# Two stacked blocks of diffusion-style layers: the order of a projection, of norms and of modulation sums is changed

## The chip, the cores and the metric

One core of a Trainium2 chip runs the whole program in one launch. The time is the device time in microseconds (us); each kernel is run three times and the median counts. Engines: TensorE (PE: matmuls; PEld: its weight loads), VectorE (DVE), ScalarE (ACT), GpSimd (POOL), SyncE (SP, which issues all DMAs here).

## What is computed

The input is an image sequence x (256 tokens of 1024), a context of the same size, and two modulation vectors c and c_ctx. The first block has two layers, the second has two layers of another kind (NSA, with its compressed keys and values, pooling, convolution and forgetting attention in four branches). Cut to what the change touches:

```python
for i in range(2):                                  # first block
    sh1, sc1, g1, sh2, sc2, g2 = split(silu(c) @ ada_w[i] + ada_b[i], 6)
    csh1, csc1, cg1, csh2, csc2, cg2 = split(silu(c_ctx) @ ada_w[i] + ada_b[i], 6)
    h  = rmsnorm(x,  norm_mix[i]) * (1 + sc1)  + sh1
    hc = rmsnorm(xc, norm_mix[i]) * (1 + csc1) + csh1
    y, yc = diff_attention(...) if i == 0 else neighbourhood_attention(...)
    x  = x + g1 * y
    x  = x + g2 * conv_ffn(rmsnorm(x, norm_ffn[i]) * (1 + sc2) + sh2)     # D_FF = 2816
    if i == 0:                                      # the context is dropped after layer 0
        xc = xc + cg1 * yc
        xc = xc + cg2 * conv_ffn(rmsnorm(xc, norm_ffn[i]) * (1 + csc2) + csh2)
x = rmsnorm(x, norm_out)
for l in range(2):                                  # second block
    proj = rmsnorm(x, norm_g[l]) @ w_in[l]          # q, kv, gates, pool, conv, fox, merge
    kc = compress(proj.k_c); vc = compress(proj.v_c)  # silu(blocks @ w1 + b1) @ w2 + b2
    ...
```

## The kernel before, in words

**Layout and precision.** The residual stream xT lies in SBUF with features on partitions: 8 chunks (kc, or m for an output block) of 128 features, 256 image columns and 256 context columns. Every large matmul is done three times on a high and a low part of both operands (`mm3` L331, `mm3r` L1055: high x high, high x low, low x high). So each weight block is loaded by SP, its high part is made by ScalarE and its low part by VectorE or GpSimd (`wload` L320, `split` L306: ScalarE at L311, the low part at L314). A count `nsplit` over all calls of `split`, with `pool_every`, picks which low parts go to GpSimd: with 3, each third one.

**Order.** A planner puts the instructions of each engine in an order of its own by a simulated timeline; the order of the program text is their priority. Three tools bind it. `keep_in_program_order` pins one instruction behind the one that the text has before it on its engine. `manual_schedule` makes the named engines issue in the order of the text. A hand-written plan (`chain` L701 with `tick`, `step`, `flush`) counts triples of matmuls: after n[0] triples it issues the mean of a norm (`norm_mean` L496), after n[1] more its broadcast (`norm_bcast` L519) and the eight scaled chunks (`norm_half`), and pins the matmuls around them.

**Norms.** The squares are made by ScalarE and added up, chunk by chunk (`norm_add` L466: square at L474, sum at L476, by the engine in "eng", the last by VectorE) or, at the front, in pairs of chunks (`norm_pairs` L479: squares at L484, three sums at L486). Two small matmuls with ones give the mean, GpSimd does the power -0.5 (L516), two more matmuls spread 1/rms over the partitions (L525), and ScalarE copies it (`nbc`). Then `norm_apply` L533 makes each chunk's scaled input: a product on VectorE (`nt`, L543), the high part on ScalarE (L544), the low part on VectorE (L545). Where the feed-forward needs the norm late, its first blocks multiply a scaled but not yet normalised input (`scale_fz` L567 into `fz`, tile v in the trace) and 1/rms is put in afterwards (`up_z` L574, `ffn` with `pre`).

**Modulation.** The six vectors per layer come in two ways. Some pieces go through TensorE in the first layer (`ada_piece` L373: 8 matmuls, a copy, two transposes, a reduce and a sum on VectorE, and a gain at L411). The other seven vectors, 56 rows of 1024 weights with two sums each (c and c_ctx), are 112 sums on VectorE (`ada_steps` L415; tile junk, L436, with a row `araw` loaded per two sums and the vectors `cb` loaded once for each feed-forward). A count of sums is given out at each up block (with 2 from block 2 on) and at each down block (3 and 4 in turn) of the feed-forward of layer 0, and what is left at the up blocks of layer 1's.

**Stages around the change.** `layer0` L721: loads, 14 warm-up matmuls, the image's norm, and the values' projection, which for each of 8 chunks adds 4 accumulators of image rows (12 matmuls of 512 columns: the triple of one accumulator before that of the next) and, from chunk 1 on, 2 of context rows; then 8 heads (`diff_head` L1096; the head's output norm ends in L1141 and the transposes at L1146), the output projection in two halves of heads (`wo` L836, the first half inside the turn of head 6), the residuals, and the norm of the feed-forward. In the second half of the output projection blocks 0 to 2 take image and context together, blocks 3 to 7 first the image, then the norm of the image, then the context (`late`). `ffn` L584 has two halves of 11 up blocks and 8 down blocks each. `layer1` L953 is the neighbourhood attention; its output projection fills `fz`, and three up blocks (`up_z`) run on it before the second feed-forward. `hybrid` L1169 is a layer of the second block; `compress_in` L1479 copies the keys and values into blocks on VectorE (`blk`, four sums), loads two weight tiles and does 32 small matmuls; `compress_out` L1510 ends the compression. Between them stands the values' projection.

## Time and profile before

| | |
|---|---|
| runs | 1619.59, 1617.31, 1611.44 us (median 1617.31) |
| the profiled execution | 1616.63 us, its span 1614.7 us, mean granted clock 0.988 |
| PE busy | 1563.8 us (97%), 10390 matmuls |
| DVE busy | 1096.7 us (68%) |
| ACT busy | 771.0 us (48%) |
| POOL busy | 527.9 us (33%) |
| HBM | 250.21 MB read, 156 GB/s over the span |

The rows below count from the start of the span. Busy times are sums of instruction times of one engine in a stretch. The granted clock (PEclk) is TensorE's clock in parts of full speed, averaged over the stretch. An arrow out<-in names the program's tiles; "x3" behind a row of a timeline is the number of like instructions drawn together.

### The profile page before, as it was taken

How to read it: one execution, taken by the hardware profiler on the slowest of the kernel's cores; microseconds unless marked ns; L12 is line 12 of the kernel's file. 1: busy time of each engine (PE TensorE's matmuls, PEld its weight loads, DVE VectorE, ACT ScalarE, POOL GpSimd, SP SyncE). 2: the span in 40 equal slices, each digit the busy share in tenths (PEclk: the TensorE clock that was granted, in tenths of full speed). 3: DMA queues.
4: the chain of work that ended last, by engine and by line, in shares of the span. 5: the costliest groups of instructions: out<-in, count | busy, mean ns of one | idle time of the engine just before them, and what ended most of it. 6: DMA issues, size and time to landing. Idle time of an engine off the chain costs nothing.

```text
span 1614.7 us, 26688 instructions
## 1 busy us (share of the span) xinstructions
PE 1563.8 (97%) x10390; PEld 1364.8 (85%) x10390; DVE 1096.7 (68%) x1927; ACT 771.0 (48%) x1386; POOL 527.9 (33%) x500
## 2 busy tenths in 40 slices
PE   7999999899999999999999987999999999999998
PEld 5777677788888888878777987999899999899998
DVE  4656677687999995343444898567657667757665
ACT  3445454454322443244545563565654445555443
POOL 2122331341100111251323654665455223552222
PEclk9999999999999999999999999999999999999999
DMA  7523233234467541243231555447335555425552
GB/s 298 218 78 128 108 131 118 83 140 169 165 212 262 209 160 61 93 153 118 96 115 35 208 186 190 183 160 260 131 106 186 207 191 208 156 92 178 188 198 90
DMA packets 49485, 252.98 MB, mean 157 GB/s; under 512 B 5072, under 2 KB 8144, under 8 KB 31568
## 3 DMA queue, kind: packets, MB, share of 16 engines
q1 hardware_dynamic: 49360, 251.28, 43.3%
q8 instruction: 82, 1.34, 0.3%
q14 instruction: 43, 0.35, 0.1%
HBM read 250.21 MB, written 1.05 MB: 156 GB/s over the span
## 4 chain that ended last, share of the span: by engine, by line
PE 86%; DVE 8%; issue 2%; ACT 2%; POOL 1%; DMA 1%; SPq 0%; DVEq 0%; POOLq 0%; ACTq 0%
PE acc L335 12%; PE acc L338 12%; PE acc L339 12%; PE S L338 9%; PE S L339 9%; PE S L335 9%; PE S L1084 3%; DVE wlo L314 2%; PE misc L383 1%; PE misc L1131 1%; PE misc L1026 1%; PE S L1058 1%; PE S L1061 1%; DVE junk L436 1%; PE S L1062 1%
## 5 line engine op out<-in xcount | busy, mean ns | idle before, releaser
L311 ACT ACTIVATE whi<-raw 128x1024 fp32r<-128x1024 f32 (+2 forms) x374 | 373.9, 1007 | 433.8 <-PE S L338 174.1
L314 DVE TENSOR_TENSOR wlo<-raw,whi 128x1024 fp32r<-128x1024 f32 (+3 forms) x305 | 373.3, 1225 | 164.8 <-ACT whi L311 164.3
L335 PE MATMUL acc<-hhi,whi 128*128 128x256 f32 (+1 forms) x824 | 271.1, 329 | 1.9 <-DVE u L618 1.4
L338 PE MATMUL acc<-hlo,whi 128*128 128x256 f32 (+1 forms) x824 | 270.9, 329 | 0.7 <-DVE hlo L545 0.6
L339 PE MATMUL acc<-hhi,wlo 128*128 128x256 f32 (+1 forms) x824 | 268.7, 327 | 1.4 <-DVE wlo L314 1.4
L314 POOL TENSOR_TENSOR wlo<-raw,whi 128x1024 fp32r<-128x1024 f32 (+1 forms) x69 | 166.5, 2414 | 193.1 <-ACT whi L311 187.8
L339 PE MATMUL S<-hhi,wlo 128*128 128x256 f32 (+1 forms) x560 | 179.5, 321 | 1.8 <-DVE wlo L314 1.8
L335 PE MATMUL S<-hhi,whi 128*128 128x256 f32 (+1 forms) x560 | 178.1, 318 | 1.4 <-ACT whi L311 1.4
L338 PE MATMUL S<-hlo,whi 128*128 128x256 f32 (+1 forms) x560 | 179.0, 320 | 0.0
L335 PEld LDWEIGHTS acc<-hhi,whi 128*128 128x128 f32 x824 | 154.9, 188 | 24.5 <-issue 9.7
L338 PEld LDWEIGHTS acc<-hlo,whi 128*128 128x128 f32 x824 | 154.9, 188 | 18.8 <-issue 5.0
L339 PEld LDWEIGHTS acc<-hhi,wlo 128*128 128x128 f32 x824 | 154.9, 188 | 15.4 <-DVE wlo L314 1.6
L436 DVE SCALAR_TENSOR_TENSOR junk<-araw,cb 128x1024 bf16<-128x1024 f32 x112 | 148.9, 1330 | 4.6 <-ACT cb L424 4.3
L624 POOL TENSOR_TENSOR u<-u,u 128x256 f32<-128x256 f32 (+1 forms) x46 | 59.2, 1288 | 273.8 <-ACT u L623 261.5
L335 PEld LDWEIGHTS S<-hhi,whi 128*128 128x128 f32 x560 | 105.9, 189 | 9.7 <-ACT whi L311 1.8
L339 PEld LDWEIGHTS S<-hhi,wlo 128*128 128x128 f32 x560 | 105.8, 189 | 9.5 <-DVE wlo L314 2.4
L338 PEld LDWEIGHTS S<-hlo,whi 128*128 128x128 f32 x560 | 105.9, 189 | 8.4
L1457 POOL TENSOR_TENSOR macc<-macc,mm 128x256 f32<-128x256 f32 x48 | 49.2, 1026 | 162.6 <-DVE mm L1455 162.6
L335 PE MATMUL acc<-hlo,whi 128*128 128x256 f32 x288 | 81.5, 283 | 1.1 <-DVE kA L1236 1.1
L338 PE MATMUL acc<-hhi,whi 128*128 128x256 f32 x288 | 81.9, 284 | 0.0
L339 PE MATMUL acc<-hlo,wlo 128*128 128x256 f32 x288 | 81.2, 282 | 0.0
L335 PE MATMUL S<-ghi,whi 128*128 128x256 f32 (+1 forms) x231 | 76.3, 333 | 4.9 <-DVE xT L638 4.8
(416 smaller groups left out, 3744.8 us busy)
## 6 DMA issues: line engine op xcount, KB each, us to landing
raw<-in_up SPq DMA_DIRECT2D x44, 1024.0 KB, 4.8
raw<-in_mg SPq DMA_DIRECT2D x32, 1024.0 KB, 5.1
araw<-in_adav SPq DMA_DIRECT2D x56, 512.0 KB, 4.3
raw<-in_t SPq DMA_DIRECT2D x24, 1024.0 KB, 4.8
raw<-in_down SPq DMA_DIRECT2D x32, 704.0 KB, 4.1
raw<-in_ada SPq DMA_DIRECT2D x16, 1024.0 KB, 4.9
raw<-in_aqk SPq DMA_DIRECT2D x8, 1024.0 KB, 5.6
raw<-in_bqk SPq DMA_DIRECT2D x8, 1024.0 KB, 4.8
```

Source lines behind the costliest of these rows:

```text
L311: nc.scalar.activation(hi[:, :n], raw, AF.Copy)
L314: eng.tensor_tensor(lo[:, :n], raw, hi[:, :n].bitcast(F32), op=ALU.subtract)
L335: first = nc.tensor.matmul(ps, wh, x[0], start=start, stop=False)
L338: nc.tensor.matmul(ps, wh, x[1], start=False, stop=False)
L339: nc.tensor.matmul(ps, wl, x[0], start=False, stop=stop)
L383: nc.tensor.matmul(ps[32 * j : 32 * j + 32, 0:256], self.cs[:, 4 * r + j, :], raw[:, 4 * r + j, :], start=(r == 0), stop=(r == 1), tile_po ...
L436: nc.vector.scalar_tensor_tensor(junk, self.araw, 1.0, self.acb[0][:, c, :], op0=ALU.mult, op1=ALU.mult, accum_out=self.ada[l][:, v, k, c ...
L624: nc.gpsimd.tensor_tensor(us[0], us[0], us[1], op=ALU.mult)
L1026: nc.tensor.matmul(o[64 * j : 64 * j + 64, :], v[:, t, (2 * h + j) * 64 : (2 * h + j) * 64 + 64], pT[:, j, t, :], start=(t == 0), stop=(t ...
L1058: first = nc.tensor.matmul(ps, x[0], w[0], start=start, stop=False)
L1084: self.nc.tensor.matmul(sps[j][:, :n], q[a][r, qs], k[b][r, ks], start=(e == 0), stop=(e == 2))
L1457: nc.gpsimd.tensor_tensor(acc, acc, m, op=ALU.add)
```

## The change

Six places. (1) The image half of xT comes in four loads instead of two. The image's norm, the first two modulation pieces and the first two chunks of the values' projection of the image rows run under `manual_schedule` on TensorE, ScalarE and VectorE; the twelve matmuls of a chunk go product by product (high x high for all four accumulators first), piece 1's transposes stand behind the first four; the low weights of chunk 0 and the sums of squares of the context half are VectorE's, and the first square of the context is pinned. `ada_piece` is cut in two for this. (2) Six of the eight output blocks of the first half of heads stand behind head 7 instead of head 6. (3) In the second half the image blocks 3 to 7 are pinned in the order of the text, and the context's scaled chunks come after 16 more triples instead of 5. (4) Before the second feed-forward, the norm is a `chain` (mean after 14 triples, the rest after 8 more), and the first two up blocks do their last two input chunks at their end. (5) All 112 sums of the modulation are given out in the first feed-forward. (6) `compress_in` stands behind the values' projection instead of before it.

```diff
...
     def ada_piece(self, p, raw=None):
+        self.ada_columns(p, *self.ada_parts(p, raw))
+    def ada_parts(self, p, raw=None):
         nc = self.nc
...
         nc.scalar.activation(part, ps[:, 0:256], AF.Copy)
+        return ps, part
+    def ada_columns(self, p, ps, part):
+        nc = self.nc
         for v in range(2):
...
         s["k"] += 1
-    def norm_pairs(self, s, x, pool, eng=None):
+    def norm_pairs(self, s, x, pool, pin=False):
         nc = self.nc
...
             sq = self.t(pool, [P, 512], "p", bufs=4).rearrange("p (e t) -> p e t", e=2)
-            nc.scalar.activation(sq, x[:, 2 * k : 2 * k + 2, :], AF.Square)
+            first = nc.scalar.activation(sq, x[:, 2 * k : 2 * k + 2, :], AF.Square)
+            if pin and k == 0:
+                self.tc.keep_in_program_order(first)
             if k:
-                (eng or nc.vector).tensor_tensor(s["pair"], s["pair"], sq, op=ALU.add)
+                nc.vector.tensor_tensor(s["pair"], s["pair"], sq, op=ALU.add)
             else:
...
         return ws, pss
+    def up_z_late(self, l, js, late):
+        res = []
+        for j in js:
+            ws = self.wload(self.i["up"][l, j], [1024, 1024])
+            pss = [self.acc5((P, T + 2)) for _ in range(2)]
+            res.append((ws, pss))
+            for which in range(2):
+                self.proj(pss[which], ws[which], self.fz[0], self.fz[1], T + 2, kcs=range(KC - late))
+        for ws, pss in res:
+            for which in range(2):
+                self.proj(pss[which], ws[which], self.fz[0], self.fz[1], T + 2, kcs=range(KC - late, KC))
+        return res
     def ffn(self, l, halves, h_hi, h_lo, sts, mid=None, pre=(), bc=None):
...
                 for jj in range(first, NFH):
                     end = up(s * NFH + jj, jj, ghi, glo)
-                    if s * NFH + jj >= 2:
+                    if l == 0:
                         self.ada_steps(fp, 2, end)
...
                     if l == 0:
-                        self.ada_steps(fp, 3 + m % 2, None)
+                        self.ada_steps(fp, 4 + s, None)
                     if s == 1 and m >= 6 and len(halves) == 2:
...
             def load_half(h):
-                for q in range(2):
-                    nc.sync.dma_start(
-                        self.xT[:, 4 * q : 4 * q + 4, T * h : T * h + T], i["xin"][h, :, 4 * q : 4 * q + 4, :]
-                    )
+                n = 2 if h == 0 else 4
+                for q in range(0, KC, n):
+                    nc.sync.dma_start(self.xT[:, q : q + n, T * h : T * h + T], i["xin"][h, :, q : q + n, :])
             stage = [self.t(hp, [P, 2, 2048], n) for n in ("ohi", "olo")]
...
             self.warm(14)
-            self.norm_pairs(sts[0], self.xT[:, :, 0:T], hp)
-            mean = self.norm_mean(sts[0])
-            self.ada_piece(0, ada[0])
-            bcs = [self.norm_bcast(self.norm_rstd(sts[0], mean)), None]
             hhi, hlo = self.new_h()
             v = self.t(hp, [P, 4128], "v")[:, 0:4096].rearrange("p (t e) -> p t e", t=4)
-            def vacc(vps, kc, w, o):
-                for (tt, hf), ps in vps.items():
-                    c = slice(tt * P, tt * P + P)
-                    f = slice(o + 512 * hf, o + 512 * hf + 512)
-                    self.mm3r(ps, (hhi[:, kc, c], hlo[:, kc, c]), (w[0][:, f], w[1][:, f]), kc == 0, kc == KC - 1)
+            def vacc(vps, kc, w, o, between=None):
+                for e, (a, b) in enumerate(((0, 0), (0, 1), (1, 0))):
+                    for (tt, hf), ps in vps.items():
+                        c = slice(tt * P, tt * P + P)
+                        f = slice(o + 512 * hf, o + 512 * hf + 512)
+                        nc.tensor.matmul(
+                            ps, (hhi, hlo)[a][:, kc, c], w[b][:, f], start=(kc == 0 and e == 0), stop=(kc == KC - 1 and e == 2)
+                        )
+                    if between and e == 0:
+                        between()
             def vout(vps, h0=0):
...
             vps = {(0, 0): self.acc(), (0, 1): self.acc(), (1, 0): self.sb(), (1, 1): self.sb(), (2, 0): self.sb(), (3, 0): self.misc()}
-            ws = []
-            for kc in range(KC):
+            bcs, ws = [None, None], []
+            front = {k: a for k, a in vps.items() if k[0] < 2}
+            with self.tc.manual_schedule(engines={nc.tensor.engine, nc.scalar.engine, nc.vector.engine}):
+                self.norm_pairs(sts[0], self.xT[:, :, 0:T], hp)
+                rstd = self.norm_rstd(sts[0])
+                parts = self.ada_parts(0, ada[0])
+                bcs[0] = self.norm_bcast(rstd)
+                self.ada_columns(0, *parts)
+                for kc in range(2):
+                    hi = self.t(self.st, [P, 1024], "whi", F32R, bufs=self.wb)
+                    lo = self.t(self.st, [P, 1024], "wlo", F32R, bufs=self.wb)
+                    ws.append((hi, lo))
+                    nc.scalar.activation(hi, avs[kc], AF.Copy)
+                    tmp = self.t(self.nrm, [P, T], "nt", bufs=5)
+                    A, B = self.nA[0][0][:, kc, 0:1], self.ada[0][:, 0, kc, 0:1]
+                    h = hhi[:, kc, 0:T], hlo[:, kc, 0:T]
+                    nc.vector.scalar_tensor_tensor(tmp, self.xT[:, kc, 0:T], A, bcs[0], op0=ALU.mult, op1=ALU.mult)
+                    nc.scalar.activation(h[0], tmp, AF.Identity, bias=B)
+                    nc.vector.tensor_tensor(lo, avs[kc], hi.bitcast(F32), op=ALU.subtract)
+                    nc.vector.scalar_tensor_tensor(h[1], tmp, B, h[0].bitcast(F32), op0=ALU.add, op1=ALU.subtract)
+                    if kc == 0:
+                        parts = self.ada_parts(1, ada[1])
+                    vacc(front, kc, ws[kc], 0, (lambda: self.ada_columns(1, *parts)) if kc == 0 else None)
+            for kc in range(1, KC):
                 if kc % 2 == 0 and kc:
...
                     avs[kc], avs[kc + 1] = raw[:, 0:1024], raw[:, 1024:2048]
-                self.pool_every = 1 if kc < 1 else 0
-                ws.append(self.split(avs[kc], 1024))
-                self.norm_half(0, 0, 0, kc, hhi, hlo, bcs[0])
-                vacc({k: a for k, a in vps.items() if k[0] < 2}, kc, ws[kc], 0)
-                if kc == 0:
-                    self.ada_piece(1, ada[1])
-                    continue
-                if kc == 1:
-                    self.norm_pairs(sts[1], self.xT[:, :, T : 2 * T], hp, nc.gpsimd)
+                if kc > 1:
+                    ws.append(self.split(avs[kc], 1024))
+                    self.norm_half(0, 0, 0, kc, hhi, hlo, bcs[0])
+                    vacc(front, kc, ws[kc], 0)
+                else:
+                    self.norm_pairs(sts[1], self.xT[:, :, T : 2 * T], hp, True)
                     bcs[1] = self.norm_bcast(self.norm_rstd(sts[1]))
...
                     wo_load(0, 1)
-                    for m in (4, 5, 6, 7):
+                    for m in (4, 5):
+                        wo(0, m, (0, 1), self.acc)
+                if h == 7:
+                    for m in (6, 7):
                         wo(0, m, (0, 1), self.acc)
...
             for m in late:
+                self.pin = True
                 wo(1, m, (0,), self.acc5)
...
             for m in late:
                 wo(1, m, (1,), self.acc5)
-            self.chain((8, 5), 0, 1, 1, sts[1], hh)
+            self.chain((8, 16), 0, 1, 1, sts[1], hh)
             pre = [self.up_z(0, 0)]
...
             hhi, hlo = self.new_h()
-            bc = self.normed(1, 1, (0,), [st2], (hhi, hlo))
-            pre = [self.up_z(1, j) for j in range(2)]
-            pre.append(self.up_z(1, 2, (self.acc5, self.misc)))
+            done = []
+            self.chain((14, 8), 1, 1, 0, st2, (hhi, hlo), done)
+            pre = self.up_z_late(1, range(2), 2)
+            pre.append(self.up_z(1, 2, (self.misc, self.misc)))
+            self.flush()
+            bc = done[0]
         if self.stop == "l1a":
...
         q = [rope2(chunk(3 + c), 0, f"q{c}") for c in range(2)]
-        part = self.compress_in(l, hp, kvT)
         vps = [self.misc() for _ in range(2)]
...
             nc.scalar.activation(vs[:, tt, :], vps[tt][:, 0:400], AF.Copy, scale=rstd[:, tt : tt + 1])
-        kcT, vc = self.compress_out(l, hp, part, wcp)
+        kcT, vc = self.compress_out(l, hp, self.compress_in(l, hp, kvT), wcp)
         gate = t(hp, [P, 2, 12], "gate")
...
```

## Rows read from the trace of the kernel before

**Rows 1.** The page, part 4: chain that ended last, by engine
```profile
PE 86%; DVE 8%; issue 2%; ACT 2%; POOL 1%; DMA 1%; SPq 0%; DVEq 0%; POOLq 0%; ACTq 0%
```

**Rows 2.** TensorE's waits: line <- releaser: us in total, times, longest
```profile
PE misc L1146 <- DVE p L1141: 4.9, 2, 3.5
PE S L335 <- DVE xT L638: 4.8, 1, 4.8
...
PE misc L525 <- POOL nrstd L516: 3.0, 2, 2.8
```

**Rows 3.** Stretches: length, busy (instructions) of PE, PEld, DVE, ACT, POOL; PEclk; DMA
```profile
10.00:24.88 14.88, 8.86 (x61) 5.77 (x61) 7.31 (x13) 6.02 (x11) 6.88 (x5) 0.89 1.03 405
24.88:38.20 13.32, 12.79 (x88) 8.60 (x88) 5.33 (x14) 4.63 (x9) 0.70 (x1) 0.87 0.64 263
285.00:310.00 25.00, 20.13 (x134) 15.47 (x134) 10.46 (x30) 8.30 (x22) 2.94 (x5) 0.86 0.31 115
325.00:333.00 8.00, 5.24 (x31) 5.24 (x32) 6.11 (x16) 3.17 (x8) 4.33 (x5) 0.79 0.36 135
880.00:910.00 30.00, 26.71 (x187) 25.03 (x188) 23.72 (x28) 16.44 (x29) 19.84 (x12) 0.89 0.38 140
930.00:937.00 7.00, 4.86 (x26) 4.45 (x26) 6.89 (x9) 5.71 (x10) 4.52 (x3) 0.76 0.05 18
955.00:1010.00 55.00, 43.79 (x326) 41.65 (x326) 49.89 (x68) 20.58 (x34) 25.46 (x14) 0.94 0.52 179
1020.00:1100.00 80.00, 80.00 (x681) 80.00 (x680) 51.11 (x82) 50.62 (x89) 51.20 (x32) 1.00 0.50 175
1120.00:1130.00 10.00, 7.74 (x85) 7.37 (x84) 9.28 (x17) 2.17 (x4) 5.74 (x7) 1.00 0.58 217
1368.00:1380.00 12.00, 10.43 (x127) 9.65 (x126) 11.91 (x22) 2.96 (x6) 7.72 (x8) 1.00 0.27 89
400.00:604.00 204.00, 204.00 (x893) 167.52 (x892) 201.37 (x305) 72.83 (x94) 20.30 (x13) 1.00 0.58 202
604.00:680.00 76.00, 76.00 (x346) 62.86 (x345) 35.21 (x53) 28.07 (x44) 14.15 (x14) 1.00 0.23 80
```

**Rows 4.** Timeline of the front: start, length, instruction, idle before it
```profile
8.26 2.29 DVE L486 TENSOR_TENSOR p<-p,p 128x512 f32<-128x512 f32 x3 [7.14 <-ACT p L484]
8.39 1.15 ACT L484 ACTIVATE p<-xT 128x512 f32<-128x512 f32 x2 [0.16 <-DMA xT<-in_xin]
...
16.41 0.16 DVE L411 SCALAR_TENSOR_TENSOR nA<-ada,vec 128x2 f32<-128x2 f32 x1
16.67 0.49 DVE L543 SCALAR_TENSOR_TENSOR nt<-xT,nA,nbc 128x256 f32<-128x256 f32 x1
...
20.04 3.96 POOL L486 TENSOR_TENSOR p<-p,p 128x512 f32<-128x512 f32 x3 [3.69 <-ACT p L484]
...
21.48 1.20 DVE L411 SCALAR_TENSOR_TENSOR nA<-ada,vec 128x2 f32<-128x2 f32 x1
22.71 1.57 DVE L543 SCALAR_TENSOR_TENSOR nt<-xT,nA,nbc 128x256 f32<-128x256 f32 x1
...
24.88 0.52 PE L1058 MATMUL acc<-whi,hhi 128*128 128x512 f32 x1 [3.84 <-ACT hhi L544]
```

**Rows 5.** Timeline of VectorE around the second feed-forward
```profile
902.09 1.57 DVE L476 TENSOR_TENSOR naccx<-naccx,nsq 128x256 f32<-128x256 f32 x1 [0.61 <-ACT nsq L474]
...
955.83 2.61 DVE L365 TENSOR_TENSOR glo<-u,ghi 128x256 fp32r<-128x256 f32 x1
```

**Rows 6.** Matmuls on the scaled input v, up to the mean (PE alone)
```profile
894.88:904.10 9.22, 7.23 (x36) 0.73 0.31 114
```

**Rows 7.** The sums (tile junk) on VectorE; each counts two instructions
```profile
380.00:500.00 120.00, 67.33 (x103) 1.00 0.56 199
500.00:620.00 120.00, 57.51 (x90) 1.00 0.53 185
940.00:1002.00 62.00, 25.00 (x32) 1.00 0.58 204
```

## The prediction

> **What bounds the kernel now.** I read the page's chain first: TensorE holds 86% of the chain that ended last, VectorE 8% [rows 1]. So no step gains by making another engine's work shorter; time can come only from places where TensorE stands still or runs at the lower of its two clock levels. I then read TensorE's waits [rows 2]: none is long (the three shown are among the four largest), and they stand at few places of the program. Last I cut the span into stretches around these places [rows 3]. Each row gives what TensorE did in a stretch and the granted clock; the row from 1020 to 1100 us is the measure of a full stage (681 matmuls of 256 columns in 80 us, 0.1175 us each, at 2.4 GHz). A granted clock of 0.87 over 13.32 us means that 2 x 0.13 x 13.32 = 3.5 us ran at 1.2 GHz, which loses at most half of that, 1.7 us. Each drop to 1.2 GHz follows a stretch with idle TensorE, so a filled gap gives back part of it too.
>
> **Part 1, the front (10 to 38 us).** Four steps.
> (a) The image half is loaded in four transfers instead of two. The last squares start when the second transfer lands, 8.39 us, and two squares and two sums follow it before the mean [rows 4]. With quarters only one square and one sum (0.6 + 0.7 us by the same rows) stand behind the last landing: 0.9 us less, if the last quarter lands when the half did. Two more issues come on SP's queue ahead of all later loads; those queue up anyway (405 GB/s from 10 us on [rows 3]), so I cost that at nothing, and keep a loss of 0.9 us, the gain turned round, as the lower end. The Trainium skill, "DMA: Bandwidth & Descriptors", section "Rules for kernel authors", asks for at least 1 MiB a transfer and speaks against this step; by it the step would give nothing, and the sum below would be 0.9 us smaller. No row here shows a quarter's landing.
> (b) Between the first and the second chunk of the values' projection TensorE stands 3.84 us, until the high part of chunk 1's input is there. Before it VectorE did a gain in 1.20 us and a product in 1.57 us; both lie under GpSimd's three sums of squares of the context half, 20.04 to 24.00 us [rows 4]. The change takes these sums off GpSimd, puts them behind chunk 1 on VectorE, and puts the transposes behind the first four of chunk 0's twelve matmuls instead of all twelve. The chain then starts 8 x 0.23 = 1.8 us earlier (0.23 us is 204 us for 893 matmuls of 512 columns [rows 3]) and is about 2 us shorter (0.16 and 0.49 us when undisturbed, at 16.41 and 16.67 us): the 3.84 us wait goes. I take 3.8 us, bounds 1.8 to 3.84. Chunk 0's weight remainder also moves from GpSimd to VectorE, behind the product and beside the first four matmuls: nothing.
> (c) The stretch that follows had the 3.5 us at 1.2 GHz [rows 3]; I take 1.0 of its 1.7 us.
> (d) The squares of the context half now stand behind chunk 1's work on ScalarE, so its mean can't come at once after the image's second chunk. Late next is therefore the context's first product. The cover is the modulation pieces 2 and 3 and the mean's own matmuls, about 4 us by that stretch. I take -0.2 us, bounds -2 to +1. Sum of part 1: 5.5 us (1.5 to 7.5). Behind it TensorE is full, so the shift stays. Two hand-written splits no longer count in the rota that gives every third split to GpSimd, so its phase changes in the heads; I cost that at 0 +- 2 us.
>
> **Part 2, the end of the first attention (285 to 310 us).** TensorE idles 4.87 us, 3.5 of them waiting for the last head's output norm [rows 2, 3], and 7 us ran at 1.2 GHz: 8.4 us lost in all. Six of the eight first-half output blocks now stand behind the last head in the program. Each is 12 matmuls of 512 columns, 6 x 12 x 0.23 = 16.6 us of work that needs no result of that head and can fill its tail. 5.0 us, bounds 0 (the planner spends them before the tail) to 8.4.
>
> **Part 3, image residuals first (325 to 333 us).** TensorE waits 2.8 us for the image's 1/rms on GpSimd [rows 2], which had context sums queued before it; with the drop, 4.4 us are lost [rows 3]. Pinning the five image blocks first ends the image's sums earlier and leaves the context's blocks as cover; the context's second norm step moves behind the whole up-projection. 3.0 us, bounds -1 (the chain waits behind other VectorE work) to 4.4.
>
> **Part 4, into the second feed-forward (880 to 937 us).** Idle 3.3 and 2.1 us and two drops, 10.4 us lost [rows 3]. The up-projection now leaves its last two input chunks to the end, so it no longer waits for them. But the mean is pinned behind 14 triples, and the sum that it needs ends at 902.09 + 1.57 = 903.66 us [rows 5]; 14 triples need only 4.9 us, so TensorE will wait for it. Until that time the present order does 36 matmuls, 12 triples [rows 6], so the gain is two, 0.7 us, and a little of the later drops: 1.0 us, bounds -2 to 5. Behind the waiting mean the whole pinned chain is queued.
>
> **Part 5, the sums of the modulation.** There are 112 sums. The loops now do 18 + 28 + 22 + 28 = 96 in the first feed-forward and 16 in the second; changed, 18 + 32 + 22 + 40 = 112 in the first, and the second loads neither vector nor rows. From 955 to 1010 us VectorE is busy 49.9 of 55 us, 25.0 us of it these 16 sums [rows 3, 7], and TensorE waits for what comes behind them (4.8 us once, for a residual [rows 2]). It did 326 matmuls there, worth 38.3 us: 16.7 us lost, its drop included. Without the sums VectorE has 24.9 us of work, less than in the full stage. I take 15.5 us, bounds 4.6 (rival 1) to 16.7. In the first feed-forward a sum costs 124.8 / 96 = 1.30 us of VectorE [rows 7], so 16 cost 20.8. VectorE is full until 604 us but idle 40.8 of the 76 us after that, with TensorE at 76 of 76 [rows 3]. The sums run ahead of their place: by 500 us 51 are done, 46 are due, 50 with the change [rows 7]. So they end later, not in TensorE's way. Eight more row loads, 4 MB, meet a stretch at 80 GB/s. Cost 0.5 us, bounds 0 to 3.
>
> **Part 6, compression late.** Twice TensorE stops before or in the compression's matmuls, 2.3 us between 1120 and 1130 and 1.6 us between 1368 and 1380 [rows 3], since its input is made on a full VectorE (9.28 of 10 us). Put behind the values' projection (48 matmuls that don't need it) these stops go; the short chain behind it then stands closer, under the scores. SP issues its weights later, still a projection ahead. 3.0 us of 3.8, bounds -1 to 3.8.
>
> **Sum.** 5.5 + 5.0 + 3.0 + 1.0 + 15.5 - 0.5 + 3.0 = 32.5 us. The profiled execution took 1616.63 us: 1584.1. The median of the runs lies 0.7 us above it: 1585.
>
> **Rivals.**
> 1. GpSimd still holds VectorE in the second feed-forward. There, a subtraction of 256 columns took 2.61 us [rows 5], five times the 0.49 us of a product of that size [rows 4]. If the two never worked together, 955 to 1010 would need 24.9 + 25.5 = 50.4 us, a gain of 4.6 instead of 15.5: 1596. Against it: from 1020 to 1100 the two are busy 51.1 and 51.2 of 80 us, so they overlap, and TensorE is full [rows 3]. The rule of that exclusion is in the Trainium skill, "SBUF — State Buffer", section "Who interferes with whom": an exclusive lock on a shared port pair; the row of 1020 to 1100 shows that it doesn't hold for every pair of instructions.
> 2. The waits of parts 2, 3, 4 and 6 are only exchanged for others, since the planner already fills what it can: 12 us less gain, 1597. For it: the waits are short and behind full VectorE queues; against it: in part 2 filler is moved, not only order.
> 3. Slower: VectorE becomes the bound of the first feed-forward. Place: 400 to 604 us, where it is busy 201.4 of 204 us. It decides where sums due overtake sums done (50 against 51 at 500 us): then they stand before the activations that free TensorE's accumulators. Price by the stretch of 955 to 1010, where this happens and 16.7 of 55 us are lost: 30% of 204 us, 62 us, so 1585 + 62 = 1647. Against it: the 51 is what spare time allowed, and by 604 us all 96 are done with 68 due.
>
> **How the numbers follow.** Forecast 0.72, rival 1 0.10, rival 2 0.13, rival 3 0.03, something else 0.02. All upper bounds of the parts together give 1571; parts 2, 3 and 6 at their lower bounds, or rival 1 or 2 with 6 us of a different plan, give 1603. Range 1571 to 1603. A change of 0.5%, 8 us, is about what a measurement of this kernel can tell from none. Forecast and rivals 1 and 2 all lie over 8 us below 1617; a mixture of both, with the lower bounds of part 1, would come within 8: faster 0.93, same 0.04, slower 0.03.
>
> **What would show it.** Right: no sums of the modulation after 700 us; TensorE full between 955 and 1010 with VectorE well below; no gap over 1 us between the first two chunks; no wait for the last head's norm; no stop before the compression. Wrong: TensorE below full between 400 and 680, a wait at the pinned mean before the second feed-forward over 4 us, or new drops of the clock.

## The result, and the profile after

The changed kernel takes 1592.38 us (median of 1592.96, 1591.89, 1592.71, 1592.05) against 1617.93 us before (four runs; the table ahead has three): a ratio of 0.985, 95% interval 0.9822 to 0.9877. That is 25.5 us less; 32.5 were forecast. The time lies in the predicted range and in its upper half. The profiled execution took 1592.96 us, span 1591.2.

The chain, as [rows 1]: VectorE's share fell, TensorE's rose.

```profile
PE 88%; DVE 6%; issue 2%; ACT 2%; DMA 1%; POOL 1%; SPq 0%; POOLq 0%; DVEq 0%; ACTq 0%
```

The stretches, as [rows 3]. Columns: start:end, length, busy (instructions) of PE, PEld, DVE, ACT, POOL, then PEclk, DMA share, GB/s. Each lies at the place in the program of a row of before, earlier by what had been gained until there; only 285 to 300 and 912 to 937 are cut otherwise.

```profile
10.00:25.00 15.00, 13.78 (x71) 9.48 (x72) 7.10 (x17) 6.14 (x11) 0.71 (x1) 0.66 1.03 413
25.00:38.00 13.00, 11.97 (x100) 7.25 (x99) 6.88 (x19) 5.42 (x12) 0.70 (x1) 0.87 0.76 299
285.00:300.00 15.00, 11.47 (x68) 8.55 (x67) 3.71 (x12) 2.82 (x7) 1.38 (x2) 0.89 0.27 91
316.00:324.00 8.00, 8.00 (x69) 7.94 (x68) 7.62 (x17) 3.80 (x11) 4.46 (x6) 1.00 0.59 207
912.00:937.00 25.00, 18.08 (x129) 16.88 (x129) 23.48 (x33) 16.84 (x31) 16.17 (x11) 0.93 0.40 139
945.00:1000.00 55.00, 55.00 (x469) 55.00 (x469) 29.94 (x47) 29.63 (x46) 30.66 (x19) 1.00 0.52 180
1100.00:1112.00 12.00, 11.41 (x80) 10.89 (x79) 11.93 (x19) 4.35 (x7) 7.13 (x7) 1.00 0.55 191
1348.00:1360.00 12.00, 12.00 (x80) 12.00 (x80) 11.38 (x20) 4.94 (x5) 7.69 (x9) 1.00 0.41 136
389.00:593.00 204.00, 204.00 (x893) 167.36 (x892) 200.52 (x304) 72.65 (x94) 21.71 (x13) 1.00 0.59 207
593.00:669.00 76.00, 76.00 (x345) 62.85 (x344) 54.99 (x86) 28.10 (x44) 14.82 (x14) 1.00 0.37 123
```

The residuals (316), the second feed-forward (945) and the first one (389, 593) are full; the first took the 16 more sums without a loss. Besides the front (10, 25), two places are far from full: the tail of the last head (285) and the way into the second feed-forward (912). The waits of TensorE there and at the start of layer 1, as [rows 2] (in us: total, times, longest):

```profile
PE misc L1197 <- DVE p L1192: 3.5, 1, 3.5
...
PE misc L515 <- DVE naccc L484: 2.1, 1, 2.1
...
PE acc L339 <- DVE wlo L314: 3.7, 2, 2.5
PE S L338 <- DVE hlo L555: 1.5, 1, 1.5
```

**Where the time came from.** Both kernels do the same matmuls (3,230,680 columns), so the two traces can be laid on each other by work: at each time of before, count the columns done until then, look up when the changed kernel had done as many, and subtract. The lead so found, worked out from the start times of all matmuls:

| time of before, us | lead, us | what lies since the line above | lead won there | forecast |
|---|---|---|---|---|
| 70 | 0.8 | front (part 1) | 0.8 | 5.5 |
| 280 | 4.6 | heads | 3.8 | 0 +- 2 |
| 310 | 7.2 | last head's end (part 2) | 2.6 | 5.0 |
| 340 | 11.2 | residuals (part 3) | 4.0 | 3.0 |
| 680 | 11.1 | first feed-forward | -0.1 | -0.5 |
| 890 | 7.6 | layer 1 | -3.5 | 0 |
| 945 | 3.2 | into the second feed-forward (part 4) | -4.4 | 1.0 |
| 1012 | 20.0 | sums taken out (part 5) | 16.8 | 15.5 |
| 1440 | 23.5 | second block (part 6) | 3.5 | 3.0 |

The last line is the difference of the spans, 1614.7 - 1591.2. The table compares one execution of each kernel, and where their order differs the count sways, since a column is not worth the same time in all matmuls. Among the profiles below, those whose engines run the same order of instructions in a stage differ there by 0.4 us (heads, 80 to 240 us), 2 us (front), 2.5 us (240 to 345 us) and up to 3.3 us (680 to 720 us), and one program run twice by 5 us between 940 and 1080 us. So a line of the front, of part 2 or of layer 1 is good to 2 or 3 us; the heads, parts 3 and 5 and the second layer of part 6 repeat within 0.5 us where the order is the same (but for one execution, see the norm chain undone).

### The profile page after: what moved, and what is told of

Same layout as the page of the kernel before. It is cut to its first block, busy times and chain, and to the rows that moved or that the text cites. A ratio compares the mean times of both kernels' runs of the same rounds, so it can differ in the third digit from the quotient of the medians.

```text
span 1591.2 us, 26696 instructions
## 1 busy us (share of the span) xinstructions
PE 1556.5 (98%) x10390; PEld 1358.1 (85%) x10390; DVE 1086.4 (68%) x1930; ACT 769.1 (48%) x1385; POOL 515.1 (32%) x496
## 4 chain that ended last, share of the span: by engine, by line
PE 88%; DVE 6%; issue 2%; ACT 2%; DMA 1%; POOL 1%; SPq 0%; POOLq 0%; DVEq 0%; ACTq 0%
PE acc L335 13%; PE acc L339 13%; PE acc L338 13%; PE S L335 10%; PE S L339 10%; PE S L338 10%; PE S L1135 3%; PE S L786 2%; PE misc L387 1%; DVE wlo L314 1%; PE misc L1077 1%; PE misc L1182 1%; PE misc L338 1%; PE misc L335 1%; PE misc L339 1%
## 5 line engine op out<-in xcount | busy, mean ns | idle before, releaser
L314 POOL TENSOR_TENSOR wlo<-raw,whi 128x1024 fp32r<-128x1024 f32 (+1 forms) x68 | 158.3, 2328 | 184.3 <-ACT whi L311 180.0
L444 DVE SCALAR_TENSOR_TENSOR junk<-araw,cb 128x1024 bf16<-128x1024 f32 x112 | 145.3, 1297 | 3.3 <-ACT cb L432 2.9
```

Of the source, the lines that this page charges most:

```text
L314: eng.tensor_tensor(lo[:, :n], raw, hi[:, :n].bitcast(F32), op=ALU.subtract)
L444: nc.vector.scalar_tensor_tensor(junk, self.araw, 1.0, self.acb[0][:, c, :], op0=ALU.mult, op1=ALU.mult, accum_out=self.ada[l][:, v, k, c ...
```

## The experiments

The same count by work is used here; "ahead" and "behind" are against the trace of the changed kernel. Ratios are to the kernel before on the same chip. Most of their intervals overlap that of the changed kernel (0.9822 to 0.9877), so what an edit costs is read from its stage in the traces, and not from the ratio.

**The sums put back.** The distribution of before in the changed kernel:

```diff
-                    if l == 0:
+                    if s * NFH + jj >= 2:
                         self.ada_steps(fp, 2, end)
...
-                        self.ada_steps(fp, 4 + s, None)
+                        self.ada_steps(fp, 3 + m % 2, None)
```

> The changed kernel with the modulation sums given out as before the change (96 in the first feed-forward, 16 in the second); all else as changed. Measured so far: between the points of work that the kernel before reaches at 945 and 1012 us, the changed kernel gains 16.8 us. Theory (the 16 sums hold up the second feed-forward): the run is 15 to 17 us slower than the changed kernel's 1592.4, about 1609, and the loss stands in that stage. Rival (VectorE stays held by GpSimd there): only 4.6 us slower, 1597. Rival (the gain came from elsewhere, such as another plan): within 2 us of the changed kernel.

Measured: 0.9926 (0.99 to 0.9952), median 1605.99 us. In the stage the lead changes from 2.3 us ahead to 9.7 behind: 12.0 us. The stretch, with columns as above:

```profile
945.00:1005.00 60.00, 52.62 (x411) 50.33 (x409) 53.99 (x73) 26.72 (x43) 29.23 (x17) 0.97 0.55 192
```

VectorE is busy 53.99 of 60 us again and TensorE is not full. The rival of 4.6 us falls; 12 is less than the 15 expected: with the sums this stage takes 62.1 us in the changed kernel against 67.0 in the kernel before, and 50.2 without them. Where the 4.8 us between the two come from was not tried.

**The sums alone.** The same two lines the other way round, in the kernel before.

> The kernel before with only the sums' distribution of the change (all 112 in the first feed-forward). Theory: 15 to 17 us faster than before, about 1601, all of it in the second feed-forward, nothing in the first. It also tells what the 4.4 us are that the changed kernel loses just ahead of that stage (between the points of 890 and 945 us of before): if they come with the pinned norm chain, this run does not lose them; if they come with the sums' removal, it does.

Measured: 0.9885 (0.9848 to 0.9923), median 1600.54 us. By work against before it is level (within 1.3 us) up to 940 us and 17.9 us ahead at 1020. So this part alone gives 16.8 us, all in the second feed-forward, nothing is lost in the first, and the 4.4 us ahead of that stage are not lost here: they come with the norm chain.

```profile
955.00:1010.00 55.00, 55.00 (x470) 55.00 (x469) 29.62 (x46) 28.47 (x42) 27.76 (x17) 1.00 0.57 191
```

Beside [rows 3] for the same 55 us: TensorE went from 43.79 to 55.00, VectorE from 49.89 to 29.62. The rows and vectors that are no longer loaded there are hardly the cause: DMA moves no less (179 GB/s before, 191 here).

**The norm chain undone.**

```diff
-            done = []
-            self.chain((14, 8), 1, 1, 0, st2, (hhi, hlo), done)
-            pre = self.up_z_late(1, range(2), 2)
-            pre.append(self.up_z(1, 2, (self.misc, self.misc)))
-            self.flush()
-            bc = done[0]
+            bc = self.normed(1, 1, (0,), [st2], (hhi, hlo))
+            pre = [self.up_z(1, j) for j in range(2)]
+            pre.append(self.up_z(1, 2, (self.acc5, self.misc)))
```

> The changed kernel with the norm before the second feed-forward as it was (no chain, the first two up blocks in one go). Theory A (the chain costs the 4.4 us): about 4 us faster than the changed kernel, 1588. Forecast of the prediction (chain worth 1.0 us): 1593.4. Rival B (the loss is VectorE held by GpSimd's subtractions, whatever the order): within 2 us of 1592.4, with VectorE over 90% busy in the stage in both.

Measured: 0.982 (0.979 to 0.9851), median 1587.47 us. From 880 to 940 us it goes from 2.6 us behind to 2.0 ahead: undoing part 4 wins 4.6 us in its stage (5.3 in the second execution below). Theory A stands, and the step of the prediction has the wrong sign. The trace of the profiled execution (1584.79 us) showed something else: from 940 to 1080 us the lead kept growing with TensorE full in both. That is the next run.

**The same kernel again.**

> The same kernel as the one with the norm before the second feed-forward undone. In that run's profile 1366 matmuls of 256 columns, from 933 to 1088 us, stood 113.3 ns apart, where all other profiles have 117.8 ns there: 6.1 us, though nothing but the order just ahead differs. Theory (the spacing is set by chance when a stretch begins, and differs between executions of one program): 117.8 ns now, and a span about 6 us longer, 1589. Rival (the program sets it): 113.3 ns again, span 1583.

Measured: 1587.93 us, span 1586.1. The stretch in the first execution and in the second:

```profile
940.00:1080.00 140.00, 140.00 (x1238) 140.00 (x1237) 96.50 (x139) 88.29 (x147) 88.15 (x55) 1.00 0.57 191
```

```profile
940.00:1080.00 140.00, 140.00 (x1191) 140.00 (x1191) 87.28 (x136) 84.85 (x142) 83.49 (x52) 1.00 0.55 187
```

Full busy and full granted clock in both, yet 1238 matmuls against 1191: 113 and 118 ns each. The order of the matmuls is the same, so the program alone does not set the spacing there; the theory of chance holds. (The span came out 3.1 us longer, not 6: the second execution was faster elsewhere by some 3 us.)

**No low parts on GpSimd on the way in.**

```diff
+            self.pool_every = 0
             self.chain((14, 8), 1, 1, 0, st2, (hhi, hlo), done)
...
+                    if l == 1 and s == 0 and jj == 5:
+                        self.pool_every = 2
```

> The changed kernel, but from the pinned norm chain to the fifth up block of the second feed-forward no low part of a weight goes to GpSimd; VectorE makes them all (1.22 us each instead of 2.3 to 2.6 on GpSimd). Theory B (VectorE waits for GpSimd's long subtractions there, an instruction of 0.47 us taking 2.3 to 2.6): the stage gains back 3 to 6 us, 1587 to 1590, though VectorE has five more subtractions to do. Rival (VectorE is simply full there, 23.5 of 25 us): five times 1.22 = 6 us more work on it make the stage slower, by up to 6 us, 1598.

Measured: 0.9829 (0.9799 to 0.9858), median 1588.54 us; 3.6 us won from 880 to 940. One long wait of TensorE for VectorE, 6.3 us, is left there. The low parts of the norm's chunks on VectorE (duration in ns: min/median/max), in the changed kernel and here:

```profile
L555 DVE SCALAR_TENSOR_TENSOR hlo<-nt,ada,hhi x6: 472/548/2631, 904.4 to 911.6; 128x256 fp32r<-128x256 f32 x6
```

```profile
L555 DVE SCALAR_TENSOR_TENSOR hlo<-nt,ada,hhi x6: 475/550/966, 902.3 to 910.0; 128x256 fp32r<-128x256 f32 x6
```

Two such holds in the changed kernel, VectorE's row and GpSimd's:

```profile
911.57 2.26 DVE L555 SCALAR_TENSOR_TENSOR hlo<-nt,ada,hhi 128x256 fp32r<-128x256 f32 x1
931.36 3.17 DVE L314 TENSOR_TENSOR wlo<-raw,whi 128x1024 fp32r<-128x1024 f32 x1
```

```profile
911.01 2.53 POOL L314 TENSOR_TENSOR wlo<-raw,whi 128x1024 fp32r<-128x1024 f32 x1
931.09 2.36 POOL L314 TENSOR_TENSOR wlo<-raw,whi 128x1024 fp32r<-128x1024 f32 x1
```

The instruction of 0.47 us ends at 913.83, just behind GpSimd's at 913.54, and TensorE waits 1.5 us for it; the one of 1.22 us ends at 934.53, 1.1 us behind GpSimd's, and TensorE waits 2.5 us for it (the waits above). This agrees with the rule of the exclusive lock in the Trainium skill, "SBUF — State Buffer", section "Who interferes with whom", for a VectorE instruction with two SBUF inputs beside a GpSimd one that reads SBUF. The rival (VectorE too full for five more subtractions) falls.

**The old front**, with its two loads, its order and its rota (the functions as they were before).

> The changed kernel with the old front: two loads of the image half, the planner's own order, the context's sums on GpSimd, and the two splits counted in the rota again. Measured so far: at the point of work that before reaches at 30 us the changed kernel leads by 2.9 us, at 70 us by 0.8, at 280 us by 4.6. Theory (the front gives 0.8 us only, since TensorE then waits for the modulation pieces, and the heads' 4 us come from the rota's phase): 4 to 5 us slower than the changed kernel in all, of it 1 us by 70 us and the rest in the heads, 1597. Forecast of the prediction (5.5 us of the front, kept to the end): 1598 with all of it by 40 us. Rival (the heads' gain is chance of another plan): about 1 us slower, 1593.5.

Measured: 0.9881 (0.9857 to 0.9906), median 1599.17 us. At 60 us it is 1.2 us ahead, at 280 us 3.3 behind, at 340 us 3.8: nothing is lost in the front, 4.4 us in the heads. The theory holds for the heads; the 1 us that it gave the front is within what executions differ by there.

**The old phase of the rota**, the front as changed:

```diff
+            self.nsplit += 2
             for kc in range(1, KC):
```

> The changed kernel with the two hand-written splits counted in the rota as before, so that the same weights' low parts as before go to GpSimd in the heads and after; the front as changed. Theory (the rota's phase makes the 4 us that are gained in the heads between 70 and 280 us): those 4 us go, 1596. Rival (they come from elsewhere): within 1.5 us of 1592.4 at 280 us.

Measured: 0.9859 (0.9838 to 0.988), median 1596.98 us; 1.9 us ahead at 80 us, 4.5 behind at 280, so 6.4 us lost in the heads, with nothing changed but the phase.

**The third phase** (the same line with 1 for 2).

> The changed kernel with one split more in the rota instead of two, the third of the three possible phases in which every third low part goes to GpSimd. The first (as changed) and the second (as before) differ by 4 to 6 us between 70 and 280 us. Theory (the old phase is the bad one: it puts GpSimd's subtractions beside the chains that TensorE waits for at one head): the third is within 2 us of the changed kernel at 280 us. Rival (the changed kernel's phase is the one good one of three): 4 to 6 us slower at 280 us.

Measured: 0.99 (0.987 to 0.993), median 1602.2 us; 0.5 us behind at 60 us, 8.7 at 280. So the rival holds: the changed kernel's phase is the best of three in the heads, and no part of the change aimed at it. All 14 profiles say so: the work of 80 to 240 us of before takes 155.2 to 155.6 us in the nine with the changed phase, 159.7 to 160.0 in the four with the old one, and 164.3 in the third. One stretch of the heads, old phase and third (the changed kernel has 30.00 of 30 there at 1.00):

```profile
195.00:225.00 30.00, 28.85 (x158) 21.63 (x157) 19.06 (x43) 15.14 (x36) 8.25 (x9) 0.89 0.37 141
```

```profile
195.00:225.00 30.00, 27.39 (x159) 20.59 (x159) 21.39 (x48) 16.72 (x39) 11.69 (x11) 0.89 0.29 109
```

TensorE is idle there for 1 to 3 us, and 2 x 0.11 x 30 = 6.6 us ran at 1.2 GHz, which cost up to 3.3 us more.

**The output blocks back at head 6.**

```diff
-                    for m in (4, 5):
-                        wo(0, m, (0, 1), self.acc)
-                if h == 7:
-                    for m in (6, 7):
+                    for m in (4, 5, 6, 7):
```

> The changed kernel with all eight first-half output blocks inside the turn of head 6 again. Measured so far: between the points of 285 and 315 us of before the change gains 2.0 us. Theory (the planner had part of this filler in the tail already): 2 us slower than changed, 1594.4, with the wait for the last head's norm back in the trace. Forecast of the prediction: 5 us, 1597.

Measured: 0.9857 (0.9835 to 0.9879), median 1595.6 us; from 0.8 us ahead at 240 us to 1.0 behind at 320, 1.7 us. Its wait for the heads' output norm is as before, two times and 4.9 us; the changed kernel still has one of them, 3.5 us (above). Of the work of 240 to 345 us of before, this run does in 101.1 us what six profiles with the part's order do in 97.9 to 100.4:

```profile
PE misc L1194 <- DVE p L1189: 4.9, 2, 3.5
```

**The residuals' pins undone.**

```diff
-                self.pin = True
                 wo(1, m, (0,), self.acc5)
...
-            self.chain((8, 16), 0, 1, 1, sts[1], hh)
+            self.chain((8, 5), 0, 1, 1, sts[1], hh)
```

> The changed kernel without the pins on the image's output blocks and with the context's second norm step after 5 triples instead of 16. Measured so far: 4.4 us gained between 320 and 340 us. Theory (order of the image blocks): 3 to 4.4 us slower, 1595.4 to 1596.8, with the wait for the image's 1/rms back. Rival (the planner now finds the order by itself): within 1 us of 1592.4.

Measured: 0.9862 (0.9841 to 0.9883), median 1596.28 us; 3.2 us lost from 280 to 360 us, and the wait for 1/rms is back:

```profile
PE misc L535 <- POOL nrstd L526: 2.1, 1, 2.1
```

**Compression early again** (`compress_in` back ahead of the values' projection).

> The changed kernel with the compression's blocks ahead of the values' projection again. Measured so far: 1.5 us gained in the first layer of the second block (1110 to 1190 us of before) and 2.0 us in its second layer (1370 to 1430). Theory (the stops in front of and in the compression go): 3.5 us slower than changed, ratio to before 0.9865, both stops back in the trace. Rival (the planner's other order in the two layers makes them): within 1 us of changed.

Measured: 0.9872 (0.9841 to 0.9902), median 1597.34 us; 3.7 us lost in the first layer and 2.0 in the second, 5.7 in all. In the first layer the stop is not the one before the compression's matmuls; TensorE waits for VectorE (kvT) in the projection ahead of them:

```profile
PE acc L335 <- DVE kvT L1295: 3.0, 1, 3.0
```

```profile
1095.00:1110.00 15.00, 12.02 (x132) 11.41 (x132) 13.67 (x25) 4.33 (x8) 7.78 (x8) 0.89 0.53 183
```

**A version from these findings.** The chain undone, no low parts on GpSimd there, and two output blocks kept for the tail of the last head, with blocks 4 to 7 all in the turn of head 6 again:

```diff
+            def tail_blocks():
+                for m in (0, 1):
+                    self.pin = True
+                    wo(0, m, (0, 1), self.acc)
...
-                self.diff_head(hp, h, q, k, v, nlam, ohi, olo)
+                self.diff_head(hp, h, q, k, v, nlam, ohi, olo, tail_blocks if h == 7 else None)
...
-                if h == 7:
                     for m in (6, 7):
...
-                    for m in (2, 3, 0, 1):
+                if h == 7:
+                    for m in (2, 3):
...
+        if tail:
+            tail()
         tp = self.misc()
```

> The changed kernel with three edits at separate stages. (1) Two first-half output blocks are pinned behind the last head's value matmuls, ahead of its transposes, so that the planner can't spend them earlier. (2) The norm before the second feed-forward as before the change. (3) From there to the fifth up block no low part of a weight on GpSimd. Theory for (1): the 3.5 us wait for the last head's norm, which the changed kernel still has, goes, and some 1 us of a clock drop behind it; the 24 pinned matmuls need 5.5 us. Rival for (1): what fills the tail is missing earlier, a new wait of the same size at head 7's softmax, gain 0 to 1 us. Theory for (2) and (3): the 4.6 us of undoing the chain and the 3.6 us of the edit (3) are for the most part one loss seen twice (VectorE held by GpSimd), so together 5 to 6 us, not 8. In all 8 to 11 us faster than the changed kernel, ratio to before 0.978 to 0.980; rival 0.982.

Measured: 0.9809 (0.9782 to 0.9836), median 1586.47 us, span 1585.2: lower than both kernels, though its interval overlaps that of the changed kernel and it is not told apart from the chain undone alone. Edits (2) and (3) together win 6.5 us from 880 to 940, against 4.6 to 5.3 and 3.6 alone: mostly one loss seen twice, as expected. Edit (1) is a miss. The tail is full, but TensorE now waits 1.4 and 0.8 us in head 7, at 266 and 268 us, and in the 15 us from 310 it is not full (beside 15.00 of 15 at 1.00 in the changed kernel):

```profile
285.00:300.00 15.00, 15.00 (x86) 11.95 (x85) 10.44 (x21) 6.65 (x13) 1.40 (x2) 1.00 0.39 141
310.00:325.00 15.00, 13.61 (x99) 13.20 (x99) 10.63 (x22) 7.08 (x15) 10.39 (x12) 0.89 0.42 144
```

Against the second execution of the kernel without the chain it goes from 0.4 us ahead at 260 us to 1.8 behind at 360. The filler taken for the tail is missing in head 7, as the rival said, and behind the tail too, where the context's mean is waited for 1.0 us: the rival, at a higher price than expected. How much of it the blocks moved back to head 6 make was not tried apart.

## Why the prediction was right, and where not

**Part 5, the largest term, was right**: 15.5 forecast, 16.8 measured alone, 12.0 by putting the sums back. The reasoning (VectorE busy 49.9 of 55 us with sums that other stretches can hold) names the cause; the first feed-forward stayed at 204.00 of 204, so rival 3 falls; with TensorE at 55.00 of 55 in the second, rival 1 as a price for the stage falls too. GpSimd's hold is real, but it cost in part 4. One reading was off: 25.0 us for the sums is [rows 7] from 940 to 1002 us; from 955 to 1010 it is 22.9, so the rest there is 27.0 and not 24.9. Nothing hangs on it.

**Part 3** (3.0) measured 3.2 to 4.0, **part 6** (3.0) 3.5 to 5.7: right in size. For part 3 the wait that was named came back with the old order. For part 6 the second layer gives 2.0 us in every profile; in the first the stop came back at another place than the one named.

**Part 4 had the wrong sign.** The step "a little of the later drops: 1.0 us, bounds -2 to 5" failed: it lost 4.4 us, and undoing it wins 4.6 to 5.3. The work of 880 to 945 us of before takes 69.4 to 71.1 us in seven profiles with the chain and 64.0 to 65.0 in four without it. I had priced the wait at the pinned mean, and it is there in the runs that keep the chain, but short: 0.2 us in the changed kernel's profile, 1.7 in others. What I did not price is the stretch behind it (912 to 937 us: 18.08 of 25, VectorE 23.48). At the same place before, VectorE is as full, and TensorE loses less:

```profile
920.00:943.00 23.00, 20.71 (x157) 19.93 (x156) 22.43 (x37) 17.44 (x32) 15.36 (x12) 0.93 0.59 231
```

From the start of the broadcast's copy (900.71 us) to the end of the last low part on VectorE (913.82) it takes 13.1 us with the chain; without it, in four profiles, 11.6. And VectorE's instructions that TensorE needs are among those held: the two shown above make 4.0 us of its waits. The run that takes GpSimd's subtractions away wins 3.6 us, so most of the loss hangs on them. But that piece from the copy to the last low part is not shorter there (13.9 us), so its length is not what cost; which piece of part 4 (pins, late input chunks, other accumulators) brings instructions and holds together was not tried.

**Part 1 was mis-sized, and its sum was saved by something else.** The 3.84 us wait did go, as step (b) said. TensorE's timeline of the changed kernel (start, length, instruction): chunk 1 follows chunk 0 at 22.50 us without a gap.

```profile
16.61 1.11 PE L387 MATMUL misc<-ohi,cs 128*32 128x256 f32 x8
17.65 1.22 PE L786 MATMUL acc<-whi,hhi 128*128 128x512 f32 x2
...
22.04 0.63 PE L786 MATMUL S<-whi,hlo 128*128 128x512 f32 x2
22.50 0.63 PE L786 MATMUL acc<-whi,hhi 128*128 128x512 f32 x2
...
25.41 1.02 PE L515 MATMUL misc<-cst,p 128*128 128x2 f32 x8
27.46 0.71 PE L535 MATMUL misc<-cst,nrstd 128*128 128x128 f32 x4 [1.03 <-POOL nrstd L526]
```

But step (a) gave nothing at the first chunk (17.65 us; 17.75 before). The last quarter came later than the half had (its square starts at 8.74 us, not 8.39), so the mean's matmuls came 0.45 us earlier and not 0.9; then the modulation pieces ahead of the chunk waited 0.6 and 0.5 us for their loads, and the second (its end is the row at 16.61) ran at 1.2 GHz. Nothing gained is what the prediction had said for the rule of the Trainium skill ("DMA: Bandwidth & Descriptors", section "Rules for kernel authors"), at least 1 MiB a transfer; no run here tells the size of the transfers from the late piece. Step (d)'s wait for the context's mean came, 1.0 us here, and step (c)'s clock drop did not go but moved: the granted clock from 10 to 25 us is 0.66, and 13.6 us up to 38 us ran at 1.2 GHz where it was 6.8 [rows 3]. The first head's projection starts at 67.3 to 70.0 us in eleven profiles with the new front, at 68.5 to 71.1 in three with the old: on the mean 1.5 us of the 5.5. The range that was put to this part, 1.5 to 7.5, was also too narrow: the lower bounds of its own steps, -0.9, 1.8 and -2, add up to -1.1 with step (c) at nothing. The step "its phase changes in the heads; I cost that at 0 +- 2 us" was the second miss: it is worth some 4.5 us there, in the changed kernel's favour. The two errors cancelled by luck, 4.6 us at 280 us for 5.5.

**Part 2** gave 2 to 2.6 us of 5.0 (0.6 to 3.1 over six profiles), by its own lower bound: "the planner spends them before the tail". It did: the last block's matmuls start at 290.3 us, and the wait begins at 291.2. The long wait of 3.5 us stayed, only the shorter one went.

**Rival 2** (waits only exchanged, 12 us less) is half right: parts 2 and 4 fell 7.8 us short of the forecast, parts 3 and 6 went 1.5 over it. Layer 1 lost 3.5 us for which there was no step, and the profiles split it in two halves. At its start an instruction of VectorE stood 2.6 us beside a GpSimd subtraction, and the context's mean came 2.1 us late: the work of 680 to 720 us of before takes 41.8 us. The order of the instructions there is the same in all profiles but that of the third phase, yet eight of these take 40.0 to 40.3 us and five 41.5 to 43.3; what decides it stays open. The other half is the rota again, which runs in layer 1 too: the work of 720 to 880 us takes 159.8 to 160.0 us in the four profiles with the old phase and 161.5 to 161.7 in the nine with the changed one. So the phase wins 4.5 us in the heads and gives 1.7 back here.

## What to carry to other kernels

Ask of each stage which engine the critical one waits for, and move its deferrable work (here sums with a due time far off) to a stage where it has slack; that paid what was forecast. Filler behind a tail is worth nothing if a planner may spend it earlier, and if it is pinned there, ask what it covered before. A rota that counts calls couples places far apart: when an edit changes the count, its phase is a change of its own and should be tried by itself, and read in every stage that the rota reaches.

## What the runs showed of the hardware that was not expected

TensorE, full and at a granted clock of 1.00, ran the same stream of matmuls of 256 columns at one of two spacings, 113.3 or 117.8 ns from start to start. Two executions of one program differ in it over a whole stage (1366 matmuls in the case above, worth 1366 x 4.5 = 6.1 us). It can also change inside an unbroken stream: in the changed kernel it is 113.4 ns from 1315 to 1337 us and 117.8 on both sides, where the matmuls take other inputs (ahi, alo), and in the run of the third phase it went from 117.8 to 113.4 at 1083 us, behind two gaps of 0.2 us. What sets it stays open; differences of this size between single executions need a second execution before they are given to an edit.

A short wait was followed by a loss of several times its length. In the old phase of the rota TensorE waited 1.1 us until 202.6 us, among small matmuls; the granted clock was 0.74 from 200 to 205 us and 0.58 from 205 to 210, which is 6.8 us at 1.2 GHz, up to 3.4 us more lost. Not every such wait is: the changed kernel waited 0.9 us once between 70 and 285 us, at a granted clock of 1.00 up to 280.
